# Loading memory tiles by SyncE all at once, and a one-hot operand in two small buffers, in a hybrid decoder layer

## The chip, the cores and the metric

The kernel runs on one core of a Trainium2 chip. The metric is the device time of one execution in microseconds (us). The engines are TensorE (PE; its weight loads are PEld), VectorE (DVE), ScalarE (ACT), GpSimd (POOL) and SyncE (SP). SP only issues transfers here; POOL issues some as well.

## The reference

One decoder layer on a sequence of 512 tokens with 1024 channels, in float32:

```
x = x + 0.5 * swiglu(rms_norm(x, norm_ffn1_w), ffn1_w_in, ffn1_w_out)
x = x + hybrid_mixer(rms_norm(x, norm_mix_w), ...)      # SSD heads and differential attention
x = x + memory_cross_attention(rms_norm(x, norm_cross_w),
                               rms_norm(mem, norm_mem_w), w_cq, w_ck, w_cv, w_co)
x = x + 0.5 * swiglu(rms_norm(x, norm_ffn2_w), ffn2_w_in, ffn2_w_out)
return rms_norm(x, norm_final_w)

swiglu(h, w_in, w_out): gate, up = split(h @ w_in);  (silu(gate) * up) @ w_out      # width 2816
attention bias:         rel_bias[rel_bucket(rel)]    # rel_bias: 32 buckets x 8 heads
```

`mem` is a fixed memory of 256 tokens with 1024 channels. Two things that the mixer and the cross-attention need long after the first feed-forward are prepared during it: the attention bias as a function of distance, and the RMS norm of the memory tokens.

## The kernel before

Tokens lie along the free dimension and channels along the 128 partitions: `x` is 8 tiles of 128 x 512. Each float32 operand of a large product is split into a high part (`...h`, made by ACT, L149 or L153) and a low part (`...l`, made by DVE, L150 or L154), and each product is three matmuls (L140, or L218 in the quads). A weight tile (`wr`, 128 x 1024, 512 KB) is loaded by SP into one of 6 buffers and split into `wh` and `wl`, of which there are 3 each.

A feed-forward (`ffn`) works in three thirds of 8, 8 and 6 hidden tiles. Each third has an input part, which makes two gate and two up tiles at a time (`quad`: seven products `qa`, `qb`, `qe` from five loaded weight tiles, two of which POOL completes by a transfer that accumulates, L226), and an output part: for each of 8 output tiles one weight tile, 3 matmuls for each hidden tile into `po`, and two DVE instructions that add the result to `x` (L448, L449). Hidden tiles end as `gh` and `gl`, by way of `gate`, `th` and ACT's and DVE's L393 to L398. The two hidden pairs of the last quad are ready only some time after the first matmuls of the output part begin.

The order of the program is written by `Order`: a dense stream of matmul work, and side chains that are woven into it by an estimate of PE's time (`od.t`); a chain's `yield n` puts its next step n us of that estimate later. When an output part of the first feed-forward begins, `beside` starts side chains: in the middle third `prepare` (the bias table and small constants) and `memory_norm`; in the last third `memory_prep`, which makes the scaled and split memory `hm` for the keys. Much later `out_attn` starts `memory_prep` again, for the values.

The order on SP is the order of the program text (`manual_schedule(engines={SP})`). For the other engines a planner orders the instructions when the program is built: it takes, by the order of the text, the first that it believes ready. On the chip each engine then runs its own list in that order and waits where it must. `issue_after`, and the helper `behind` around it, put an instruction behind a named one on its engine.

Small tiles come from one pool with two tags: tiles of more than 256 columns take one of 56 buffers (`s2`), others one of 14 (`s1`):

```
def s2(s, dt=F32, shape=(P, T)):
    if math.prod(shape[1:]) <= T // 2:
        return sp.tile(list(shape), dt, tag="s1", name=nm(s), bufs=NHALF)
    return sp.tile(list(shape), dt, tag="s2", name=nm(s))
```

`prepare` (L486 to L514) loads `lamv`, `rel_sb` (the 32 x 8 bias values) and `hot` (32 x 512, one-hot rows that pick a bucket for each distance) by SP. After 7.5 us of the estimate it multiplies them on PE (`prel`, 8 x 512), copies the result over `hot` on ACT (L511), stores it by POOL to `rel_d` (L512) and has POOL write it 128 times to `rel_z` (L514), from which each attention head reads its bias.

`memory_tile` (L870) loads one 128 x 256 tile of the memory by POOL, behind the last accumulating transfer of the text. `memory_norm` loads such a tile, squares it on ACT (`nacc`, `nsq`) and adds the square on DVE (L339), 8 times with 2 us between; `finish` then makes the norm with small matmuls `nps` and `nrow`. `memory_prep` loads each tile again and splits it into `hm`.

Of the kernel before, what the change touches and what calls it, by code (L numbers as in the profile page):

```python
# [13 lines left out]
AF = mybir.ActivationFunctionType  # L14
# [4 lines left out]
T = 512  # L19
D = 1024  # L20
KT = D // P
# [6 lines left out]
NUM_BUCKETS = 32  # L28
# [66 lines left out]
def body(tc, a, dbg=None):  # L95
    nc = tc.nc
# [12 lines left out]
    def nm(s):  # L109
        uid[0] += 1  # L110
        return f"{s}_{uid[0]}"
# [5 lines that stand above are left out]
# [4 lines left out]
    def small(s, n, bufs=None):  # L121
        return tiny.tile([P, n], F32, tag=s, name=nm(s), bufs=bufs)

    def acc(s, shape=(P, T)):
        return acc_p.tile(list(shape), F32, tag="acc", name=nm(s))

    def aux(s, shape=(P, T)):
        return aux_p.tile(list(shape), F32, tag="aux", name=nm(s))
# [5 lines left out]
    last, start, last_sum, recent = [], [], [], []  # L134
    V, S, G = nc.vector, nc.scalar, nc.gpsimd
    od = Order()

    def mm(out, w, x, start, stop):
        od.t += (1 if w.dtype == R32 else 4) * (x.free_size() + 8) / 2400
        nc.tensor.matmul(out, w, x, start=start, stop=stop)  # L140
# [16 lines left out]
    def split(s, src, scale=None, half=False, n=T):  # L157
        if half:
            both = s2(s, R32, (P, 2, T // 2))
            hi, lo = both[:, 0], both[:, 1]  # L160
        else:
            hi, lo = s2(s + "h", R32, (P, n)), s2(s + "l", R32, (P, n))
        last[:] = [i.ins for i in split_into(hi, lo, src, scale)]
        return hi, lo

    def load_w(src, n=D):
        raw = wp.tile([P, n], F32, tag="wr", name=nm("wr"), bufs=6)
        nc.sync.dma_start(raw, src)
        hi = wp.tile([P, n], R32, tag="wh", name=nm("wh"))
        lo = wp.tile([P, n], R32, tag="wl", name=nm("wl"))  # L170
        with ExitStack() as after:
            for i in start:
                after.enter_context(tc.issue_after(i))
            recent[:] = [i.ins for i in split_into(hi, lo, raw)]
        return hi, lo

    @contextmanager
    def behind(ins):
        with ExitStack() as after:
            for i in ins:  # L180
                after.enter_context(tc.issue_after(i))
            yield

    H = T // 2
# [87 lines left out]
    def proj(ps, w, xs, ks=None):  # L272
        n = len(xs)
        for k in ks or range(n):
            mm3(ps, w, xs[k], k == 0, k == n - 1, wc=slice(k * P, (k + 1) * P))
            yield
# [187 lines left out]
    def beside(ti):  # L464
        if ti == 1:
            od.spawn(prepare())
            od.spawn(memory_norm())
        elif ti == 2:
            od.spawn(memory_prep(hm))

    def fin1(o):
        st_mix.add(x[o])
# [2 lines left out]

    od.spawn(st1.finish(), 18.0)
    od.add(ffn(h1, [], st1, a["f1q"], [a["f1o0"], a["f1o1"], a["f1o2"]], fin1, wa_s, a["f1i"], at_out=beside))


# [3 lines left out]
    rel_d = dram.tile([8, RW], F32, name="rel_d")  # L483
    rel_z = dram.tile([8, P, RW + 1], F32, name="rel_z")

    def prepare():  # L486
        lamv = cp.tile([P, 4, 64], F32, name="lamv")
        yield 0.0
        nc.sync.dma_start(lamv, a["lam"].partition_broadcast(P))
        lamp = small("lamp", 64, bufs=2)  # L490
        lsum = small("lsum", 2, bufs=1)
        for j in range(2):
            V.tensor_tensor(lamp, lamv[:, 2 * j, :], lamv[:, 2 * j + 1, :], ALU.mult)
            V.reduce_sum(lsum[:, j : j + 1], lamp, axis=AX.X)
        lexp = small("lexp", 2, bufs=1)
        G.tensor_tensor(lexp, euler[:, 0:1].to_broadcast([P, 2]), lsum, ALU.pow)
        V.tensor_tensor(nlam, lexp[:, 1:2], lexp[:, 0:1], ALU.subtract)
        V.tensor_scalar(nlam, nlam, -LAMBDA_INIT, None, ALU.add)
        V.tensor_scalar(wsub, par[:, C_SUBLN : C_SUBLN + 1], 1.0 - LAMBDA_INIT, None, ALU.mult)
        V.tensor_scalar(dskh, par[:, C_DSKIP : C_DSKIP + 8], 0.5, None, ALU.mult)  # L500
        rel_sb = s2("rel_sb", shape=(NUM_BUCKETS, 8))
        nc.sync.dma_start(rel_sb, a["rel_bias"])
        hot = s2("hot", shape=(NUM_BUCKETS, T))
        nc.sync.dma_start(hot, a["hot"])
        rel_far = s2("rel_far", shape=(8, RW - T))
        V.memset(rel_far, MASKED)
        nc.gpsimd.dma_start(rel_d[:, T:], rel_far)
        yield 7.5
        prel = aux("prel", (8, T))
        mm(prel, rel_sb, hot, True, True)  # L510
        S.activation(hot[:8], prel, AF.Copy, scale=-8.0)  # L511
        nc.gpsimd.dma_start(rel_d[:, :T], hot[:8])  # L512

        nc.gpsimd.dma_start(rel_z[:, :, :RW], rel_d[:, None, :].to_broadcast([8, P, RW]))  # L514

# [187 lines left out]

    def out_attn(hg, o0, o1, prep=False):
        if prep:
            od.spawn(memory_prep(hm2), 0.0)
        yield lambda: all(y is not None for y in ya[4 * hg : 4 * hg + 4])
        heads = ya[4 * hg : 4 * hg + 4]
        for o in range(o0, o1):
            po = acc("pm")  # L710
            yield from proj(po, load_w(a["woa"][hg, o], 4 * P), heads)
            V.tensor_tensor(x[o], x[o], po, ALU.add)
        if o1 == KT:
            ya[4 * hg : 4 * hg + 4] = [None] * 4
# [152 lines left out]
    st_mem = Stat(MEM)  # L867
    ck, cv = [], []

    def memory_tile(k):  # L870
        mk = s2("mem", shape=(P, MEM))
        with behind(last_sum):
            nc.gpsimd.dma_start(mk, a["memT"][k])
        return mk

    def memory_norm():
        for k in range(KT):
            mk = memory_tile(k)
            with behind(recent):
                st_mem.add(mk)  # L880
            yield 2.0
        yield 3.0
        yield from st_mem.finish(6.0)

    def memory_prep(dst):
        for k in range(KT):
            mk = memory_tile(k)
            with behind(recent):
                dst.append(split("hm", mk, par[:, C_MEM + k : C_MEM + k + 1], True))
            yield 2.0  # L890
# [51 lines left out]
    hm, hm2 = [], []  # L942
# [4 lines left out]
    for hd in range(1, 4):  # L947
        od.add(queries_keys(hd))
    od.add(group_dense(0))
    od.add(out_attn(0, 0, 8))  # L950
    od.add(values(1))
    for hd in range(4, 8):
        od.add(queries_keys(hd))
    od.add(group_dense(1))
    od.add(out_attn(1, 0, SPLIT))
    od.add(group_dense(2))
    od.add(group_dense(3))
    od.add(out_attn(1, SPLIT, 8, True))
    od.add(memory_values())
    od.add(out_proj(ys, a["wos"], lambda: all(y is not None for y in ys), upd_c))  # L960
# [221 lines left out]
```

## Time and profile before

| | |
|---|---|
| median of 3 runs | 1351.1 us (1350.3 to 1351.55) |
| the profiled execution, whole | 1348.26 us |
| the profiled execution, span from first to last instruction | 1346.1 us |
| mean granted clock of TensorE | 0.998 |
| PE busy | 1321.8 us, 98% |
| DVE, ACT, POOL busy | 950.7, 631.2, 114.0 us |
| the 8 loads of `wr` of the middle third's output part, first and last issue on SP | 194.5 and 233.0 us |
| `hot`: issue of its load; its store to `rel_d`; `rel_z` | 195.9; 231.1; 233.5 us |
| memory tiles, POOL: first load of the norm; first of `hm` | 198.3; 314.2 us |

Every row of the trace is from the one profiled execution. A timeline row gives the start, the duration, the engine, the line, the operation and the tiles it writes and reads; in brackets stands the idle time of that engine before it and what ended it. A row of waits gives a total, a count and the longest. Matmuls are pipelined: the next begins before the last has ended, and their ends are modelled.

### The profile page before, as it was taken

The numbers are of one execution on the slowest core, as the hardware profiler recorded it, in microseconds if no ns is written. First come the engines' busy times: TensorE is split into PE (matmuls) and PEld (weight loads), VectorE is DVE, ScalarE is ACT, GpSimd is POOL, SyncE is SP. The second block draws the span as 40 slices with busy tenths as digits, with TensorE's granted clock in tenths as the row PEclk, the third lists the DMA queues.
The fourth block names the chain that finished last, engine by engine and source line by source line (L and its number), as shares of the span: only waits on it lengthen the run. The fifth ranks groups of instructions, "written<-read, shape, count | busy, mean of one in ns | idle before, by whom it ended". The sixth has DMA issues, their size and how long they took to land.

```text
span 1346.1 us, 19858 instructions
## 1 busy us (share of the span) xinstructions
PE 1321.8 (98%) x7829; PEld 1148.1 (85%) x7829; DVE 950.7 (71%) x1480; ACT 631.2 (47%) x1069; POOL 114.0 (8%) x138
## 2 busy tenths in 40 slices
PE   8999998999999999999999999999999999999997
PEld 7888997889897778877788887889889989998996
DVE  6774787467895586657867877656788757875774
ACT  6442454145553474446654555434445424542453
POOL 1000011111020001100011031000011000000000
PEclk9999999999999999999999999999999999999999
DMA  7434574756442314432162574322347655745641
GB/s 268 111 119 128 128 198 121 229 126 184 126 150 80 99 33 83 138 96 67 45 132 84 92 137 146 110 78 64 81 113 182 174 129 126 200 140 125 172 111 62
DMA packets 50540, 167.89 MB, mean 125 GB/s; under 512 B 6592, under 2 KB 7000, under 8 KB 50448
## 3 DMA queue, kind: packets, MB, share of 16 engines
q1 hardware_dynamic: 40704, 134.57, 31.8%
q0 software_dynamic: 9744, 32.06, 14.2%
q8 instruction: 61, 1.00, 0.3%
q14 instruction: 31, 0.25, 0.1%
HBM read 164.45 MB, written 4.77 MB: 126 GB/s over the span
## 4 chain that ended last, share of the span: by engine, by line
PE 88%; DVE 4%; DMA 2%; ACT 2%; issue 1%; POOL 1%; POOLq 0%; SPq 0%; ACTq 0%; DVEq 0%
PE po L140 16%; PE qb L218 11%; PE pm L140 8%; PE qe L218 7%; PE qa L218 7%; PE pxbc L140 7%; PE pk L140 3%; PE pq L140 3%; PE pcq L140 3%; PE pv L140 3%; PE pz L140 3%; PE pf L140 2%; PE pg L140 2%; PE pu L140 2%; PE ps L140 2%; DMA r<-cum_d 2%
## 5 line engine op out<-in xcount | busy, mean ns | idle before, releaser
L149 ACT ACTIVATE wh<-wr 128x1024 fp32r<-128x1024 f32 (+2 forms) x285 | 292.1, 1027 | 384.0 <-PE po L140 117.9
L150 DVE TENSOR_TENSOR wl<-wr,wh 128x1024 fp32r<-128x1024 f32 (+2 forms) x285 | 337.6, 1185 | 101.1 <-ACT wh L149 98.8
L140 PE MATMUL po<-gh,wh 128*128 128x512 f32 x304 | 118.6, 392 | 2.8 <-ACT wh L149 1.6
L140 PE MATMUL po<-gh,wl 128*128 128x512 f32 x304 | 118.0, 390 | 0.5 <-DVE wl L150 0.5
L140 PE MATMUL po<-gl,wh 128*128 128x512 f32 x304 | 118.2, 390 | 0.2 <-DVE gl L150 0.2
L218 PE MATMUL qa<-hmh,wl 128*128 128x256 f32 x304 | 86.3, 284 | 0.1
L218 PE MATMUL qa<-hml,wh 128*128 128x256 f32 x304 | 86.1, 283 | 0.0
L218 PE MATMUL qa<-hmh,wh 128*128 128x256 f32 x304 | 86.0, 283 | 0.0
L448 DVE TENSOR_TENSOR upd<-po,row 128x512 f32<-128x512 f32 x40 | 27.6, 691 | 78.6 <-PE po L140 78.3
L140 PEld LDWEIGHTS po<-gh,wh 128*128 128x128 f32 x304 | 56.8, 188 | 17.3 <-ACT gh L149 3.2
L140 PEld LDWEIGHTS po<-gl,wh 128*128 128x128 f32 x304 | 57.1, 188 | 12.9 <-DVE gl L150 1.3
L140 PEld LDWEIGHTS po<-gh,wl 128*128 128x128 f32 x304 | 57.1, 188 | 12.5 <-DVE wl L150 1.0
L218 PEld LDWEIGHTS qa<-hmh,wl 128*128 128x128 f32 x304 | 58.3, 192 | 0.7 <-DVE wl L150 0.7
L218 PEld LDWEIGHTS qa<-hml,wh 128*128 128x128 f32 x304 | 58.3, 192 | 0.2
L218 PEld LDWEIGHTS qa<-hmh,wh 128*128 128x128 f32 x304 | 58.3, 192 | 0.2
L140 PE MATMUL pxbc<-hnh,wh 128*128 128x512 f32 x128 | 52.3, 408 | 0.0
L140 PE MATMUL pxbc<-hnl,wh 128*128 128x512 f32 x128 | 50.3, 393 | 0.0
L140 PE MATMUL pxbc<-hnh,wl 128*128 128x512 f32 x128 | 50.2, 393 | 0.0
L226 POOL DMA_DIRECT2D wr<-in_f2q x22 | 19.2, 871 | 362.3 <-DVE wl L150 86.7
L636 ACT ACTIVATE ec<-ec,mn 128x512 f32<-128x512 f32 (+3 forms) x64 | 35.4, 555 | 25.2 <-DVE mn L635 25.2
L218 PE MATMUL qe<-s12h,wh 128*128 128x256 f32 x152 | 43.4, 286 | 3.2 <-ACT wh L149 1.9
L149 ACT ACTIVATE gh<-th 128x512 fp32r<-128x512 f32 x38 | 23.1, 624 | 45.7 <-DVE th L396 45.7
(375 smaller groups left out, 3808.0 us busy)
## 6 DMA issues: line engine op xcount, KB each, us to landing
wr<-in_f2q SPq DMA_DIRECT2D x55, 512.0 KB, 3.9
wr<-in_f1q SPq DMA_DIRECT2D x40, 512.0 KB, 4.3
wr<-in_f2q POOLq DMA_DIRECT2D x22, 512.0 KB, 6.3
wr<-in_f2o SPq DMA_DIRECT2D x22, 512.0 KB, 4.4
wr<-in_f1q POOLq DMA_DIRECT2D x16, 512.0 KB, 5.8
wr<-in_f1o SPq DMA_DIRECT2D x16, 512.0 KB, 4.2
wr<-in_wxbc SPq DMA_DIRECT2D x16, 512.0 KB, 3.5
wr<-in_f1i SPq DMA_DIRECT2D x8, 512.0 KB, 6.9
```

The source lines that it names most:

```text
L140: nc.tensor.matmul(out, w, x, start=start, stop=stop)
L149: S.activation(hi, src, AF.Copy),
L150: V.tensor_tensor(lo, src, hi.bitcast(F32), ALU.subtract),
L218: nc.tensor.matmul(out, a_[:, wc], b_, start=first and f == 0 and kp == 0 and j == 0, stop=kp == n - 1 and j == 2, skip_group_check=True)
L226: last_sum[:] = [G.dma_start(raw, m, accum_op=ALU.add).ins]
L448: V.tensor_tensor(upd, po, row4, ALU.mult)
L636: S.activation(ec[:, :n], ec[:, :n], AF.Exp, bias=mn, scale=-1.0, accum_out=sm[c][:, i : i + 1])
```

## The change

`memory_tile` takes the issuing queue as an argument and no longer stands behind the last accumulating transfer. `memory_norm` loads all 8 tiles by SP before its first step, then waits 2 us of the estimate ahead of each square instead of behind it. `memory_prep` loads all 8 by SP at its start when it is called in the last third (`early`); at its later call it loads one at a time by POOL as before, without the place behind the accumulating transfer. `hot` becomes two tiles of 32 x 256, which by their size take the tag `s1`; product, copy and store are made for each half, and `rel_z` is written once both are stored.

```diff
@@ beside
-            od.spawn(memory_prep(hm))
+            od.spawn(memory_prep(hm, True))
@@ prepare
-        hot = s2("hot", shape=(NUM_BUCKETS, T))
-        nc.sync.dma_start(hot, a["hot"])
+        hot = [s2("hot", shape=(NUM_BUCKETS, H)) for _ in range(2)]
+        for i in range(2):
+            nc.sync.dma_start(hot[i], a["hot"][:, i * H : (i + 1) * H])
...
         prel = aux("prel", (8, T))
-        mm(prel, rel_sb, hot, True, True)
-        S.activation(hot[:8], prel, AF.Copy, scale=-8.0)
-        nc.gpsimd.dma_start(rel_d[:, :T], hot[:8])
+        for i in range(2):
+            mm(prel[:, i * H : (i + 1) * H], rel_sb, hot[i], True, True)
+        for i in range(2):
+            S.activation(hot[i][:8], prel[:, i * H : (i + 1) * H], AF.Copy, scale=-8.0)
+            nc.gpsimd.dma_start(rel_d[:, i * H : (i + 1) * H], hot[i][:8])
@@ out_attn
-            od.spawn(memory_prep(hm2), 0.0)
+            od.spawn(memory_prep(hm2, False), 0.0)
@@ memory
-    def memory_tile(k):
+    def memory_tile(k, queue):
         mk = s2("mem", shape=(P, MEM))
-        with behind(last_sum):
-            nc.gpsimd.dma_start(mk, a["memT"][k])
+        queue.dma_start(mk, a["memT"][k])
         return mk
 
     def memory_norm():
-        for k in range(KT):
-            mk = memory_tile(k)
+        mem = [memory_tile(k, nc.sync) for k in range(KT)]
+        for mk in mem:
+            yield 2.0
             with behind(recent):
                 st_mem.add(mk)
-            yield 2.0
         yield 3.0
         yield from st_mem.finish(6.0)
 
-    def memory_prep(dst):
+    def memory_prep(dst, early):
+        mem = [memory_tile(k, nc.sync) for k in range(KT)] if early else []
         for k in range(KT):
-            mk = memory_tile(k)
+            mk = mem[k] if early else memory_tile(k, G)
```

## The prediction

> **What bounds the kernel now.** The first view is the page. TensorE (PE) carries the span.
>
> ```profile
> span 1346.1 us, 19858 instructions
> PE 1321.8 (98%) x7829; PEld 1148.1 (85%) x7829; DVE 950.7 (71%) x1480; ACT 631.2 (47%) x1069; POOL 114.0 (8%) x138
> ```
>
> PE is idle for 1346.1 - 1321.8 = 24.3 us. A change that only moves loads and small copies can win no more than the part of this idle time that lies in its own stages, plus PE's own slow restarts there. The second view is the table of windows: two output parts and two runs of quads, each cut from the end of one stage to the end of the next. After the stage's bounds stand its length, PE's busy time and records, then PEld, DVE, ACT, POOL, clock, DMA share and GB/s.
>
> ```profile
> 221.83:270.99 49.16, 45.65 (x196) 35.88 (x196) 24.03 (x30) 11.62 (x14) 7.05 (x10) 1.00 0.58 173
> 1073.13:1117.02 43.89, 43.88 (x195) 35.88 (x194) 24.48 (x29) 10.65 (x12) 2.60 (x3) 1.00 0.52 131
> 270.99:336.87 65.88, 62.57 (x512) 61.50 (x511) 50.32 (x59) 32.46 (x43) 9.32 (x13) 1.00 0.57 156
> 1117.02:1177.50 60.48, 60.48 (x507) 60.48 (x506) 47.41 (x50) 30.24 (x36) 4.32 (x5) 1.00 0.65 167
> ```
>
> Rows 1 and 2 are the same work, the output part of a full third, in the first and the second feed-forward; only the first has the bias table and the memory norm beside it. It takes 49.16 - 43.89 = 5.27 us more: 49.16 - 45.65 = 3.51 us of idle PE and 45.65 - 43.88 = 1.77 us of extra busy time. Rows 3 and 4 are three quads each; here the first feed-forward loses 5.40 us: 3.31 us idle and 2.09 us extra busy. The clock column is 1.00 in all four, so no throttle is in this. The third view is who PE waited for from 221 to 336 us (total, times, longest):
>
> ```profile
> PE qe L218 <- ACT wh L149: 1.9, 1, 1.9
> PE po L140 <- ACT wh L149: 1.6, 1, 1.6
> PE po L140 <- ACT gh L149: 1.1, 1, 1.1
> PE qe L218 <- DVE wl L150: 0.8, 1, 0.8
> PE qb L218 <- DVE wl L150: 0.5, 1, 0.5
> PE po L140 <- DVE wl L150: 0.5, 1, 0.5
> PE po L140 <- DVE gl L150: 0.2, 1, 0.2
> ```
>
> Seven waits, and they are all the idle time of both stages: the `po` rows sum to 3.4 us (output part), the `qe` and `qb` rows to 3.2 us (quads). All end on splits made by ACT and DVE, none on a DMA. So the question is why ACT split late. The fourth view is ACT's timeline, first around the output part that begins at 221.83, then at the same place in the second feed-forward (1073.13):
>
> ```profile
> 209.73 1.04 ACT L149 ACTIVATE wh<-wr 128x1024 fp32r<-128x1024 f32 x1
> ...
> 215.98 1.06 ACT L149 ACTIVATE wh<-wr 128x1024 fp32r<-128x1024 f32 x1 [1.82 <-PE qb L218]
> 216.94 0.40 ACT L335 ACTIVATE nacc<-mem 128x256 f32<-128x256 f32 x1
> 217.25 0.40 ACT L338 ACTIVATE nsq<-mem 128x256 f32<-128x256 f32 x1
> 222.64 1.06 ACT L393 ACTIVATE th<-gate 128x1024 f32<-128x1024 f32 x1 [4.99 <-DVE gate L392]
> 226.38 1.15 ACT L149 ACTIVATE gh<-th 128x512 fp32r<-128x512 f32 x2 [2.67 <-DVE th L396]
> 230.20 0.59 ACT L511 ACTIVATE hot<-prel 8x512 f32<-8x512 f32 x1 [2.67 <-PE prel L140]
> 230.70 1.04 ACT L149 ACTIVATE wh<-wr 128x1024 fp32r<-128x1024 f32 x1
> ```
>
> ```profile
> 1070.17 1.06 ACT L149 ACTIVATE wh<-wr 128x1024 fp32r<-128x1024 f32 x1 [1.82 <-PE qe L218]
> 1073.05 1.06 ACT L149 ACTIVATE wh<-wr 128x1024 fp32r<-128x1024 f32 x1 [1.82 <-PE qb L218]
> 1074.02 1.04 ACT L393 ACTIVATE th<-gate 128x1024 f32<-128x1024 f32 x1
> ```
>
> In the second feed-forward ACT goes on splitting weight tiles at every product's end until `th` runs at 1074.02; PE then has a second output tile to work on while the last two `g` tiles are made. In the first, after the split at 215.98 (weight tile 0) ACT stands idle for 4.99 us and splits tile 1 only at 230.70, behind the copy `hot<-prel`. The tile was there: SP issued it at 197.35, right behind `hot`.
>
> ```profile
> 195.32 0.43 SPq L502 DMA_DIRECT2D rel_sb<-in_rel_bias  x1
> 195.85 0.36 SPq L504 DMA_DIRECT2D hot<-in_hot  x1
> 197.35 0.35 SPq L168 DMA_DIRECT2D wr<-in_f1o  x1
> ```
>
> So this is an order fixed when the program was built, not a late transfer. SP's order is written by hand; those of ACT, DVE, PE and POOL come from the planner, which takes the first instruction that it believes ready. It believed `hot` and the tile behind it to come late. My reading: tiles of one tag get their buffers in program order, `hot` has the large tag, and its turn comes only after the `gh` and `gl` of the last quad (226 to 228 us). On the chip the buffer was free at 195.85; in the plan SP stood still there. The last view is POOL:
>
> ```profile
> 201.82 1.17 POOL L873 DMA_DIRECT2D mem<-in_memT  x2
> 231.08 0.53 POOL L512 DMA_DIRECT2D rel_d<-hot  x1 [28.09 <-ACT hot L511]
> 231.60 0.56 POOL L873 DMA_DIRECT2D mem<-in_memT  x1
> 233.55 1.10 POOL L514 DMA_DIRECT2D rel_z<-rel_d  x1 [1.39 <-DMA rel_d<-hot]
> ```
>
> POOL stood 28.09 us before the store of `hot`, and memory tile 3 and all later ones stood behind it (231.60 and on). The last four squares therefore fell into the first quad of the next third:
>
> ```profile
> 273.90 0.58 ACT L248 ACTIVATE qb<-qa 128x512 f32<-128x512 f32 x1 [12.91 <-PE qa L218]
> 274.39 0.41 ACT L338 ACTIVATE nsq<-mem 128x256 f32<-128x256 f32 x1
> 274.70 1.05 ACT L149 ACTIVATE wh<-wr 128x1024 fp32r<-128x1024 f32 x1
> ```
>
> **The change part by part.** (1) `hot` in two halves of the small tag, which has 14 buffers: 2 `hot`, `rel_sb`, `rel_far` and 8 memory tiles are 12, and `nacc` and one `nsq` make 14, so SP finds a buffer for each load at once, and later squares wait for one add of `nacc` at most. `hot` no longer queues behind the last quad's tiles. I expect ACT to split tiles 1 and 2 ahead of `th`, as in the second feed-forward. This removes the 3.51 us of idle time. PE's extra busy time there is 1.77 us, of which the table's product has 1.0:
>
> ```profile
> L140 PE MATMUL prel<-hot,rel_sb 32*8 32x512 f32 x2 | 1.0, 589 | 0.0
> ```
>
> The other 0.77 us are slow first matmuls after each wait and go with the waits: together -4.28 us. If the waits stay, 0.
>
> (2) The product in two halves: the same columns through PE in twice the instructions. Its cost is between 0 (time by columns) and +1.0 us (each half as dear as a whole); nearest is the whole's own 1.0 us, which is mostly streaming, so I take +0.1. ACT makes a second copy (at most the 0.59 of the whole) and POOL a second store (at most 0.53): `rel_z` starts up to 1.1 us later. Its first reader is the bias load of the first attention head, after the whole last third, so not before 336.87 (row 3 of the windows): nothing on the path.
>
> (3) Memory tiles, 8 at the first call and 8 at the second, leave POOL for SP and stand between weight tiles 0 and 1 of their output part.
>
> Eight tiles of 128 x 256 floats are 1.05 MB. Queued behind them on SP is weight tile 1 and all later ones. SP's issues of small tiles stand about 0.5 us apart (195.32 and 195.85), so eight take 4 us, and the bytes take 1.05 MB / 253 GB/s = 4.1 us at the rate of the first row here (bounds, length, clock, DMA share, GB/s):
>
> ```profile
> 194.00:200.00 6.00, 1.00 0.85 253
> 206.00:212.00 6.00, 1.00 0.14 25
> ```
>
> Tile 1 would be issued near 201 instead of 197.35; its own 512 KB take 2 us at that rate, and with the 4.1 us ahead of it it lands near 208. ACT can take it one product of PE after the split at 215.98, at about 218.9 (2.88 us, the step from 1070.17 to 1073.05). Some ten us of cover hide it; the DMA engines are nearly empty from 206 to 212 (second row). If the cover were gone, 4 us. On POOL the accumulate of the last quad's fifth tile, split at 209.73, runs beside these loads and may land up to 4.1 us later. Its product begins here (critical chain):
>
> ```profile
> 213.18 2.88 PE qb L218 x24
> ```
>
> The split ends at 210.77 on ACT and, with as much again for DVE's half, near 212; 1.2 us of slip are free, and the cost lies between 0 and 4.1 - 1.2 = +2.9; I take 0, because the DMA engines fall idle from 206 on, so most of the slip is made up. At the second call the same loads stand in the same place of SP's order, and PE is busy throughout that output part today: 0.
>
> ```profile
> 336.87:370.00 33.13, 33.13 (x148) 27.01 (x147) 28.11 (x43) 17.03 (x27) 0.00 (x0) 1.00 0.41 126
> ```
>
> [...]
>
> (4) Squares and adds of the memory norm, 2 us later in the plan but with data present: all eight move into the output part, where ACT is busy 11.62 of 49.16 us. The `nsq` at 274.39 no longer stands before the split at 274.70 (0.3 us), and DVE loses its adds of `nacc` there: between 0 and the 3.31 us of idle time of the quads; I take 0.5, because the larger cause, `qb<-qa` ahead of that split, is not touched for certain. The norm's own matmuls on PE move with it and cost the same.
>
> Sum: -4.28 + 0.1 - 0.5 = -4.7 us. The profiled execution took 1348.26 us (span 1346.1 and 2.2 around it); the median of the three runs is 1351.1, 0.2% above. A difference in PE's idle time carries over to either, so 1351.1 - 4.7 = 1346.4 us.
>
> **The rivals.** Both stages heal: the split at 274.70 stands behind `qb<-qa` because the planner believes the accumulate of the quad's second tile late, behind `rel_z` and a memory tile on POOL. With the memory tiles gone, and if the earlier `hot` lets the product run in a gap of the last quads so that `rel_z` starts sooner, the quads also run without waits: 3.31 instead of 0.5, and some 0.6 of restarts (0.77 went with four waits, here there are three): -4.28 + 0.1 - 3.9 = -8.1, 1343.0 us. For it: the quads from 1117.02 have no idle time at all. Against it: `rel_z` may start when it does now.
>
> No change: the cause of the late split is another than the buffer of `hot` (for that: SP issued it at 195.85 with no visible wait), or the planner still holds tile 1 late. Then 3.51 us of waits stay and only the 0.5 and 0.1 count: 1350.7 us.
>
> Slower: one mechanism, weight tile 1 behind eight memory loads. If the planner reckons these loads slow enough that tile 1 comes to it after the start of `po`, ACT's order puts its split behind the copies and the squares, and PE stands as in the second row of the waits, but longer. It decides once the split is planned later than today's 230.70; the price is the 4.1 us of bytes or 4 us of issues ahead of it, with the 0.1 and the 0.5: +3.7, 1354.8 us. For it: 4 us more stand in front of a tile that was late already. Against: the 10 us of cover.
>
> **How the numbers follow.** Forecast (1346.4) 0.34; both heal (1343.0) 0.27; no change 0.23; slower 0.16. A measurement here can tell 0.2%, 2.7 us, from no change. The first two are faster by more than that, 0.61; no change gives 0.23; slower 0.16. The range goes from 1342.6, just under the second case, to 1352.5, which takes in no change with 1.8 us of the accumulate's slip; it leaves out the slower case and a little on either side, about 0.2.
>
> **What would show it.** Right: in the output part of the middle third, splits of tiles 1 and 2 before `th`, no PE wait on `wh` or `gh`, the stage at 44.5 to 46.5 us (the norm's matmuls now within); `prel` in twice the instructions for about 1.1 us; all memory loads on SP within 5 us near 196; eight squares before 260. In the first quad of the last third either `qb<-qa` still ahead of the split (forecast) or behind it (both heal). Wrong: a split of tile 1 that still follows the copy of `prel`; SP waiting before a memory load; or waits of PE on `wh` after 290 that are not there today.

## The result, and the profile after

The changed kernel took 1341.48 us (median of nine runs, 1339.06 to 1346.57); nine runs of the kernel before had a median of 1349.21 us (1346.61 to 1353.36). The ratio is 0.9947, with an interval of 0.9927 to 0.9967: 7.7 us less between the medians. The forecast was 4.7 us less. Of the 4.9 us between 1346.4 and 1341.48, 1.9 are the starting point (1351.1 from three runs, 1349.21 from nine); 3.0 are the effect. One of the executions below, of the run with the memory part alone, took 1855.58 us at a mean clock of 0.654 and is left out of its ratio.

The profiled execution after took 1342.28 us. The page, in the lines that answer to the first two of before:

```profile
span 1340.4 us, 19873 instructions
PE 1321.4 (99%) x7831; PEld 1149.7 (86%) x7831; DVE 951.1 (71%) x1480; ACT 631.5 (47%) x1070; POOL 104.0 (8%) x123
```

The span lost 5.7 us and PE's busy time only 0.4. The windows of the three stages, each cut at the first matmul of the next (length, PE's busy time, then PEld, DVE, ACT, POOL, clock, DMA share, GB/s):

```profile
222.76:267.18 44.42, 44.42 (x199) 36.34 (x197) 24.26 (x34) 11.07 (x15) 1.60 (x2) 1.00 0.49 156
267.18:332.16 64.98, 62.56 (x507) 62.14 (x506) 49.05 (x54) 31.16 (x38) 5.03 (x6) 0.97 0.63 165
332.16:365.14 32.98, 32.98 (x146) 26.88 (x145) 28.03 (x42) 16.84 (x26) 0.00 (x0) 1.00 0.41 126
```

The output part of the middle third went from 49.16 to 44.42 us and has no idle time left. The quads went from 65.88 to 64.98, with a clock of 0.97 where it was 1.00. PE's waits from 221 to 336 us are two instead of seven:

```profile
PE qe L218 <- ACT wh L149: 1.7, 1, 1.7
PE qe L218 <- DVE wl L150: 0.8, 1, 0.8
```

ACT's timeline at the start of that output part shows the cause of the first gain: weight tiles 0, 1 and 2 are split at 217.08, 219.96 and 222.84, one at the end of each product, all ahead of `th`.

```profile
217.08 1.06 ACT L149 ACTIVATE wh<-wr 128x1024 fp32r<-128x1024 f32 x1 [1.82 <-PE qb L218]
218.05 0.40 ACT L335 ACTIVATE nacc<-mem 128x256 f32<-128x256 f32 x1
219.96 1.06 ACT L149 ACTIVATE wh<-wr 128x1024 fp32r<-128x1024 f32 x1 [1.51 <-PE qe L218]
220.93 0.71 ACT L338 ACTIVATE nsq<-mem 128x256 f32<-128x256 f32 x2
222.84 1.07 ACT L149 ACTIVATE wh<-wr 128x1024 fp32r<-128x1024 f32 x1 [1.21 <-PE qb L218]
223.81 1.04 ACT L393 ACTIVATE th<-gate 128x1024 f32<-128x1024 f32 x1
```

SP issued the loads as forecast, and POOL, which had stood 28.09 us before the store of `hot`, now stands 5.49; PE multiplies the table in the last quad, in four instructions and 1.03 us (two and 1.0 before):

```profile
196.57 0.88 SPq L505 DMA_DIRECT2D hot<-in_hot  x2
197.50 5.58 SPq L875 DMA_DIRECT2D mem<-in_memT  x8
```
```profile
204.43 1.03 PE L140 MATMUL prel<-hot,rel_sb 32*8 32x256 f32 x4
```
```profile
208.19 1.09 POOL L515 DMA_DIRECT2D rel_d<-hot  x2 [5.49 <-ACT hot L514]
```

In the first quad of the last third no square is left, but `qb<-qa` still stands ahead of the split on which PE waits 1.7 us:

```profile
270.25 0.58 ACT L248 ACTIVATE qb<-qa 128x512 f32<-128x512 f32 x1 [12.92 <-PE qa L218]
270.74 0.38 ACT L350 ACTIVATE row<-nrow 128x256 f32<-128x256 f32 x1
271.00 1.06 ACT L149 ACTIVATE wh<-wr 128x1024 fp32r<-128x1024 f32 x1
```

Behind that wait the clock falls (2 us windows, columns as above):

```profile
270.00:272.00 2.00, 0.45 (x4) 0.24 (x3) 0.00 (x0) 1.75 (x3) 1.60 (x2) 1.00 0.33 33
272.00:274.00 2.00, 1.13 (x5) 0.92 (x6) 1.87 (x2) 0.06 (x1) 0.00 (x0) 0.76 1.00 182
274.00:276.00 2.00, 2.00 (x11) 2.00 (x11) 0.82 (x2) 1.33 (x2) 0.00 (x0) 0.50 1.05 201
276.00:278.00 2.00, 2.00 (x17) 2.00 (x17) 2.00 (x2) 1.04 (x2) 0.00 (x0) 0.89 0.58 113
278.00:280.00 2.00, 2.00 (x19) 2.00 (x18) 2.00 (x3) 1.19 (x2) 0.00 (x0) 1.00 0.04 8
```

Missing clock times length, (0.24 + 0.50 + 0.11) x 2, is 1.7 us. In the stages of the layer's traces drops came to 1.7 us or to two or three times that (1.70 in the quads of the run with `hot` alone, 3.42 with the halves alone, 5.1 with the squares put back). Below, "less a drop" means that all of it is taken off: these quads took 64.98 - 1.70 = 63.3 us, and 65.88 before, where no drop fell. That is a lower bound: by my reading a late split catches up while the matmuls are slow. The run with the memory part alone (below) has the same matmuls in the same order in these quads, and no drop: it takes 64.21 us. So this drop cost about 0.8 us here, not 1.7, and the quads gained 65.88 - 64.21 = 1.67 us, not 2.6.

### The profile page after: what moved, and what is told of

It is laid out like the page before. It is cut to its first block, busy times and chain, and to the rows that moved or that the text cites. A ratio compares the mean times of both kernels' runs of the same rounds, so it can differ in the third digit from the quotient of the medians.

```text
span 1340.4 us, 19873 instructions
## 1 busy us (share of the span) xinstructions
PE 1321.4 (99%) x7831; PEld 1149.7 (86%) x7831; DVE 951.1 (71%) x1480; ACT 631.5 (47%) x1070; POOL 104.0 (8%) x123
## 4 chain that ended last, share of the span: by engine, by line
PE 91%; DVE 3%; DMA 1%; ACT 1%; issue 1%; POOL 1%; POOLq 0%; ACTq 0%; DVEq 0%
PE po L140 17%; PE qb L218 12%; PE qe L218 8%; PE pm L140 8%; PE qa L218 8%; PE pxbc L140 7%; PE pk L140 3%; PE pq L140 3%; PE pcq L140 3%; PE pv L140 3%; PE pz L140 3%; PE pf L140 2%; PE pg L140 2%; PE pu L140 2%; PE ps L140 2%; DMA r<-cum_d 1%
## 5 line engine op out<-in xcount | busy, mean ns | idle before, releaser
L218 PE MATMUL qe<-s12h,wl 128*128 128x256 f32 x152 | 43.8, 288 | 0.8 <-DVE wl L150 0.8
```

The costliest lines, as they stand in the source:

```text
L218: nc.tensor.matmul(out, a_[:, wc], b_, start=first and f == 0 and kp == 0 and j == 0, stop=kp == n - 1 and j == 2, skip_group_check=True)
```

## The experiments

Theory A: the plan holds `hot` until the buffers of the large tag have gone round, and with it the loads behind it on SP, so the split of weight tile 1 is planned late. Rival B: the memory tiles on POOL, stuck behind the store of `hot`, are to blame. Theory C: the split in the first quad is planned late because its tile's accumulate stands behind `rel_z` on POOL. The plan itself is not recorded: what it held is inferred from the order that each engine then ran.

**`hot` alone, with a buffer of its own.** The kernel before, and only the buffer changed (one large buffer fewer pays for it):

```diff
-NSLOT = 56
+NSLOT = 55
-        hot = s2("hot", shape=(NUM_BUCKETS, T))
+        hot = sp.tile([NUM_BUCKETS, T], F32, tag="hot", name=nm("hot"), bufs=1)
```

> Kernel before with one edit: hot stays one tile of 512 columns but has a buffer of its own (the large tag has 55 instead of 56); memory tiles stay on POOL. Theory A (the plan held hot, and the weight tiles behind it on SP, until hot's turn for a buffer of the large tag came): the output part of the middle third loses its 3.5 us of idle time and comes to 43.9 to 44.5 us instead of 49.16; the whole is 4 to 5 us faster than before. Rival B (the memory tiles on POOL and their squares made the splits late): the output part stays near 49 us and the time within 1 us.

Measured: 1344.19 us against 1350.55, ratio 0.9958 (0.9942 to 0.9975). The output part and the quads:

```profile
223.30:267.24 43.94, 43.93 (x195) 35.89 (x193) 22.14 (x27) 9.54 (x10) 5.95 (x9) 1.00 0.63 182
267.24:334.48 67.24, 63.92 (x511) 62.91 (x510) 52.31 (x62) 33.52 (x45) 8.43 (x13) 0.97 0.57 156
```

No idle time in the output part, with all memory tiles still on POOL. The quads, less a drop of 1.70, take 65.54: hardly a gain there. The whole gained 6.4 us, more than the 4 to 5 expected; the stages give 5.2, less 0.3 for the table's product in the quads before.

**`hot` in halves alone.** The kernel before with the change's edits to `prepare` and nothing else.

> Kernel before with the hot part of the change alone: two halves in small buffers, memory tiles still by POOL. Theory A: as with a buffer of its own, output part 43.9 to 44.5 us, 4 to 5 us faster. If the halving itself matters (more instructions, or the small tag filling up), it differs from the kernel with a buffer of its own by over 1 us. Rival B: output part near 49 us.

Measured: 1344.55 us against 1350.55, ratio 0.995 (0.9934 to 0.9966); output part 43.89 us, quads 68.25 less two drops of 3.42 together, 64.83. For the output part it does not matter which buffer `hot` gets, only that it has one free. In this trace the quads before the output part took 83.27 us, 1.5 more than with a buffer of its own, with a PE wait of 1.1 us on a small tile (`nlam`); the medians of the two runs differ by 0.4 us only.

**The memory part alone.** The changed kernel with `hot` as before.

```diff
-        hot = [s2("hot", shape=(NUM_BUCKETS, H)) for _ in range(2)]
+        hot = s2("hot", shape=(NUM_BUCKETS, T))
...
```

> The change without its hot part: memory tiles by SP all at once, hot one tile of the large tag. Theory A: the wait of SP for hot stays in the plan, so the output part keeps 3 to 4 us of idle time and 48.5 to 50 us; only the squares leave the quads, gain 0.5 to 1.5 us. Rival B: the output part comes to 44.5 us and the gain is 4 us or more.

Measured: 1348.58 us (1348.32 without the execution of 1855.58) against 1350.55, ratio 0.9983 (0.9966 to 1.0), so the time alone does not tell it clearly from the kernel before. Output part and quads, then ACT at the start of the output part:

```profile
222.26:273.86 51.60, 47.79 (x201) 37.48 (x199) 26.14 (x36) 13.41 (x20) 3.29 (x4) 0.97 0.45 144
273.86:338.07 64.21, 61.55 (x507) 60.92 (x506) 49.02 (x54) 31.05 (x38) 5.04 (x6) 1.00 0.67 167
```
```profile
216.58 1.06 ACT L149 ACTIVATE wh<-wr 128x1024 fp32r<-128x1024 f32 x1 [1.82 <-PE qb L218]
223.25 1.06 ACT L393 ACTIVATE th<-gate 128x1024 f32<-128x1024 f32 x1 [5.61 <-DVE gate L392]
...
230.81 0.59 ACT L511 ACTIVATE hot<-prel 8x512 f32<-8x512 f32 x1 [2.67 <-PE prel L140]
...
231.61 1.04 ACT L149 ACTIVATE wh<-wr 128x1024 fp32r<-128x1024 f32 x1
```

The split of tile 1 still follows the copy of `prel`, as before. Rival B falls, and A stands. But the quads, without a drop, take 64.21: the memory part is worth 1.67 us there, where I had put 0.5. Of the third wait of before, 0.5 us on `wl`, this row is left:

```profile
283.42 0.39 PE L218 MATMUL qa<-hmh,wh 128*128 128x256 f32 x1 [0.23 <-ACT wh L149]
```

And the old waits of the output part cost a drop in this trace (51.60 - 1.72 = 49.88), which they did not in the one I forecast from.

**The squares put back.** The changed kernel, the loads untouched, with the last four squares ordered behind `qb<-qa` of the first quad:

```diff
-        for mk in mem:
-            yield 2.0
-            with behind(recent):
+        for k, mk in enumerate(mem):
+            yield 40.0 if k == 4 else 2.0
+            with behind(recent if k < 4 else mark):
...
-        S.activation(b_ps, a_ps, AF.Copy)
+        mark[:] = [S.activation(b_ps, a_ps, AF.Copy).ins]
```

> The changed kernel with the loads as they are, but the last four squares of the memory norm ordered behind the copy qb<-qa of the last third's first quad, where the kernel before had them. Theory: these squares and the end of the norm behind them are what the quads gained by the memory part of the change; the quads take 65 to 66.5 us (63.3 in the changed kernel, 65.9 before; stretches of low clock taken out), the output part stays at 43.9 to 44.5, and the median is 1.5 to 3 us above the changed kernel's. Rival: it was the loads leaving GpSimd, not the squares; then the quads stay at 63.3 us and the median does not move.

Measured: 1345.15 us, against 1343.27 for the changed kernel and 1350.49 for the kernel before on the same chip; ratio to before 0.9958 (0.9941 to 0.9975). The quads, and PE's waits in both stages:

```profile
266.76:337.50 70.74, 65.41 (x511) 64.53 (x510) 51.98 (x59) 32.49 (x42) 4.81 (x6) 0.93 0.55 144
```
```profile
PE nps L140 <- DVE nacc L339: 3.0, 1, 3.0
PE nrow L140 <- DVE ndiag L322: 1.8, 1, 1.8
PE qe L218 <- DVE wl L150: 0.5, 1, 0.5
```

The quads take 65.6 us less drops (63.3 in the changed kernel) and have 5.3 us of waits instead of 2.4, on the squares' sum (`nacc`) and the end of the norm. The forecast number came, but by other waits than those of the kernel before: it had none on `nacc`, none on `ndiag` of this length, and the wait on `wh` is gone here. So the run shows that the place of the squares alone can cost the quads this much; it does not rebuild what the kernel before lost, and does not rule out the rival, the loads. (Low clock that lay in the 5.3 us of idle time is taken off with the rest, so the 65.6 is a lower bound.)

**Four other places for `rel_z`.** First behind the accumulate on POOL:

```diff
+        yield 50.0
+        with behind(last_sum):
-        nc.gpsimd.dma_start(rel_z[:, :, :RW], ...)
+            nc.gpsimd.dma_start(rel_z[:, :, :RW], ...)
```

> The changed kernel with the 2.6 MB write rel_z put behind the accumulating transfers of the next quad on POOL (50 us later in the plan). Theory C (the first quad of the last third waits because the plan believes the accumulate of its second tile late behind rel_z): the 2.4 us of idle time of the quads go, the quads come to 61 to 62.5 us instead of 65 (60.5 and the norm's matmuls), and the whole is 2.5 to 4 us faster than the changed kernel. Rival D (the norm's row copy and POOL's wait for the norm make the split late): the idle time stays at 2 us or more and the time is that of the changed kernel within 1 us.

Measured: 1343.81 us against 1350.55, ratio 0.9957 (0.9938 to 0.9976). In the first quad the split now runs before `qb<-qa` and PE does not wait, as C says. But the quads keep 4.2 us of idle time and take 64.17 us less two drops, so C's numbers (no idle time, 61 to 62.5 us, 2.5 to 4 us faster than the changed kernel's 1341.48) did not come. The second quad has a wait of 3.8 us on `wh`, and ACT shows why:

```profile
288.98 1.06 ACT L393 ACTIVATE th<-gate 128x1024 f32<-128x1024 f32 x1 [5.55 <-DVE gate L392]
291.13 0.58 ACT L248 ACTIVATE qb<-qa 128x512 f32<-128x512 f32 x1 [1.09 <-PE qa L218]
292.72 1.15 ACT L149 ACTIVATE gh<-th 128x512 fp32r<-128x512 f32 x2 [1.01 <-DVE th L396]
293.77 1.04 ACT L149 ACTIVATE wh<-wr 128x1024 fp32r<-128x1024 f32 x1
```

ACT idles 5.55 us before `th` while the split stands behind `th`, the copy and both `gh` in its list; POOL had issued that tile's accumulate at 283.02. My reading, not tested by itself: the second quad's accumulates now follow `rel_z` in the plan, so their tile is believed late there.

Then `rel_z` on SP, so that no accumulate stands behind it:

```diff
-        nc.gpsimd.dma_start(rel_z[:, :, :RW], ...)
+        nc.sync.dma_start(rel_z[:, :, :RW], ...)
```

> The changed kernel with the broadcast rel_z issued by SyncE instead of GpSimd. Theory: the copy qb<-qa stands ahead of the split in the first quad because the plan holds the accumulate of the second weight tile behind rel_z on GpSimd; with rel_z gone from that queue the split comes first, no PE wait on wh or wl is left in the last third's quads, they take 60.5 to 61.5 us instead of 63.3 (stretches of low clock taken out), and with fewer gaps for the clock to fall in the median is 2.5 to 4 us below the changed kernel's. Rival: the lateness only moves on, as in the run with rel_z behind the accumulate, where PE then waited 3.8 us in the second quad; quads 63 to 65 us and the same median. Second rival: SyncE waits for the stores of the table ahead of rel_z and weight tiles 2 and on come late: PE waits on wh in the output part, 46 us or more instead of 44.4.

Measured: 1339.55 us, 1343.27 for the changed kernel beside it; ratio to before 0.9907 (0.9888 to 0.9926). Output part and quads:

```profile
222.71:269.84 47.13, 45.18 (x201) 36.42 (x199) 27.37 (x39) 12.29 (x17) 4.16 (x5) 1.00 0.67 184
269.84:330.31 60.47, 60.47 (x505) 60.47 (x504) 46.26 (x49) 29.95 (x36) 2.59 (x3) 1.00 0.59 161
```

The quads take 60.47 us, as in the second feed-forward (60.48): `rel_z` on POOL was the cause of the wait. By which way is not shown. In this run and the three others of this group the end of the norm moved as well: ACT made `row` at 259.65 us here and at 257.06 to 257.80 in the others, against 270.74 in the changed kernel, where it stood right ahead of the late split. So the accumulate (C) and the norm's copy (rival D of the run before) are not told apart. The second rival holds as well: tile 2 stood behind `rel_z` on SP (8 x 128 x 640 floats, 2.6 MB), ACT waited 5.26 us for its load, and the output part is 47.13.

```profile
233.88 1.06 ACT L149 ACTIVATE wh<-wr 128x1024 fp32r<-128x1024 f32 x1 [5.26 <-DMA wr<-in_f1o]
```

Then `rel_z` on SP behind the quads' tiles (`yield 80.0` ahead of it):

> As the run with rel_z on SyncE, but with rel_z issued only behind the weight tiles of the last third's quads, so that no weight tile of either stage stands behind it. Theory: PE has no wait in the output part of the middle third nor in the quads behind it; 43.9 to 44.5 us and 60.5 us; nothing else moves, since the first reader of rel_z comes after the last output part; median 2 to 3 us below the run with rel_z on SyncE and about 6 below the changed kernel's, 1336 to 1338 us. Rival: rel_z is 2.6 MB and now lies ahead of the last output part's tiles on SyncE; if they come late PE waits there, 35 us or more instead of 33.0, and the time is no better than with rel_z on SyncE (1339.5).

Measured: 1345.13 us, far from the 1336 to 1338 expected, against 1350.59; ratio 0.9959 (0.9946 to 0.9971). Output part 44.64; PE does not wait inside the quads, but 6.49 us at their end, for the first weight tile of the next output part, whose split has moved behind `th` and `gh`:

```profile
329.44 1.06 ACT L393 ACTIVATE th<-gate 128x1024 f32<-128x1024 f32 x1 [8.48 <-DVE gate L392]
333.18 1.15 ACT L149 ACTIVATE gh<-th 128x512 fp32r<-128x512 f32 x2 [2.67 <-DVE th L396]
334.23 0.83 ACT L149 ACTIVATE wh<-wr 128x768 fp32r<-128x768 f32 x1
```

The rival named the place; on the chip SP had issued the tile at 302.09. And last, `rel_z` on SP amid the output part's tiles (`yield 20.0`):

> The changed kernel with rel_z on SyncE between the fifth and the sixth of the output part's late weight tiles (of eight), so that the tiles behind it have two or three products of PE before they are needed, and no tile of the next output part stands behind it. Theory: both earlier placements failed only by the tile that stood right behind rel_z; here the output part takes 43.9 to 44.6 us and the quads 60.5, the last output part 33.0, PE waits on no split from 221 to 365 us, and the median is 1336 to 1338.5 us, below the first placement on SyncE (1339.5). Rival: 2.6 MB ahead of two tiles and of the first quad's five again push one of them late; then PE waits on wh near the end of the output part or in the first quad and the time is 1339 or more.

Measured: 1339.23 us; the changed kernel beside it 1340.25 (below); ratio to before 0.9921 (0.9903 to 0.994). Quads 60.48, but the output part 48.76, with a drop of 1.72 and two waits. The time is above the 1336 to 1338.5 expected. The cause is neither the theory's nor the rival's: ACT stood 16.23 us at the norm's `row`, with three splits behind it.

```profile
257.06 0.38 ACT L350 ACTIVATE row<-nrow 128x256 f32<-128x256 f32 x1 [16.23 <-PE nrow L140]
257.34 2.94 ACT L149 ACTIVATE wh<-wr 128x1024 fp32r<-128x1024 f32 x3
```

The first and the last placement on SP are at or just under the changed kernel, by 3.7 and 1.0 us between medians of six; the intervals of their ratios to before overlap with the changed kernel's, so neither is shown to beat it.

**The changed kernel again.** Twice more, beside the runs above.

> The changed kernel itself, on the chip of the next runs, for comparison. Its span is read stage by stage after taking out the stretches in which the granted clock was below 1.00; in the profiles so far each such stretch costs 1.7 us or twice that. Expected: output part of the middle third 44.4 us, quads of the last third 63.3 us without such stretches, PE waits of 1.7 and 0.8 us in the first quad; median 1341 to 1344 us. If the gain of the first comparison were mostly luck of the clock, it is above 1345.

Measured: 1343.27 us against 1350.49, ratio 0.9933 (0.9913 to 0.9953); output part 44.39, quads 66.37 less two drops of 3.42 together, 62.95.

> The changed kernel once more on the same chip, as the measure for the run beside it: median 1341 to 1344 us; without stretches of low clock the output part 44.4 and the quads 63.0 to 63.3 us.

Measured: 1340.25 us against 1349.12, ratio 0.9934 (0.991 to 0.9958); output part 44.41, quads 65.14 less 1.70, 63.44. The median is just under the 1341 to 1344 expected. The gain comes again both times, so it is not mostly luck of the clock; how much of it the clock gives is worked out below.

**Gaps and the clock.** Two kernels that compute nothing of the layer, one execution of each: dense runs of matmuls (128x512), gaps between them made by chains of ACT copies.

> Not the layer: only 99 dense runs of 40 to 55 matmuls (128x512, 9 to 12 us) with a gap behind each, made by a chain of ScalarE copies on which the next run waits; eleven lengths of gap from about 0.5 to 4.5 us, nine times each in random order. Read: after which gaps the granted clock falls, and for how long. [...] Second rival: the drops have nothing to do with gaps and fall anywhere.

> Not the layer: dense runs of matmuls and gaps as in the ladder of gaps, with seven kinds of gap, fourteen times each: single ones of about 1.7, 1.9 and 2.1 us, and pairs with two matmuls (0.5 us) between them, about 1.7 and 0.75, 1.25 and 1.25, 1.0 and 1.0, 0.64 and 0.64 us. In the ladder no gap up to 1.73 us lowered the clock, while 7 of 9 of 2.2 to 2.3 us did; in the layer it fell behind a pair of 1.67 and 0.76 us. [...] Rival: only one unbroken gap counts; then no pair lowers the clock. [...]

One drop of the ladder: the matmuls with the gap before them, then the clock in 2 us windows.

```profile
388.96 12.78 PE L80 MATMUL ps<-h,wr 128*128 128x512 f32 x48 [2.28 <-ACT h L85]
```
```profile
388.00:390.00 2.00, 1.04 (x4) 0.90 (x5) 0.88 (x2) 0.00 (x0) 0.97 0.00 0
390.00:392.00 2.00, 2.00 (x6) 1.53 (x5) 0.00 (x0) 0.00 (x0) 0.50 0.04 8
392.00:394.00 2.00, 2.00 (x8) 1.60 (x7) 0.00 (x0) 0.00 (x0) 0.68 0.00 0
```

The missing clock adds to (0.03 + 0.50 + 0.32) x 2 = 1.7 us. Counted over both kernels:

| gap, us | drops behind it |
|---|---|
| 0.37 to 1.57 | 0 of 53 |
| 1.67 to 1.73 | 0 of 23 |
| 1.77 to 1.83 | 7 of 14 |
| 2.06 to 2.12 | 7 of 14 |
| 2.22 to 2.28 | 7 of 9 |
| 2.5 | 5 of 9 |
| 2.86 to 3.2 | 6 of 9 |
| 3.95 to 4.01 | 9 of 9 |
| pair 0.64 and 0.64, 0.5 of matmuls between | 1 of 13 |
| pair 1.0 and 1.0 | 5 of 14 |
| pair 1.25 and 1.25 | 9 of 14 |
| pair 1.73 and 0.75 | 8 of 14 |

No drop stood behind the 76 single gaps of 0.37 to 1.73 us, and 9 of 9 had at least one at 3.95 to 4.01; in between it was 5 to 7 of each 9 or 14. Of the pairs, those of 1.0 us and more had a drop in 5, 9 and 8 of 14 cases, though no gap in them is longer than 1.73 us: the rival that only one unbroken gap counts is out (the one drop at 0.64 and 0.64 stands by itself; its second gap had grown to 0.92). Drops that fall anywhere are out as well, by the same 76. What in the chip brings a drop about is not shown.

## Why the prediction was wrong

The largest term, the output part, was right in mechanism and size. The time came out below the range because the quads' term (4) was priced by the wrong rows, a term for the clock was missing, and the base was high.

(1) "Together -4.28 us" for the output part: right. It lost 4.74 us, and 0.33 of it came back in the quads before (81.44 to 81.77 us), where the table's product went: -4.4. The runs with `hot` alone show it by itself (43.94 and 43.89 us), and the run without it shows the old waits.

(2) +0.1 for the halves: 1.03 us in four instructions for 1.0 in two. Right.

(3) 0 for the loads on SP: right. No tile came late, and the last output part took 32.98 us (33.13). Eight issues took 5.58 us, against the estimate of 4.

(4) "The norm's own matmuls on PE move with it and cost the same", and the 0.5 us taken for the rest: this step failed. Without a drop the quads gained 1.67 us. Most of it is the norm's own matmuls, which in the kernel before stood amid the quads' products:

```profile
283.67 0.60 PE L140 MATMUL nps<-ones,nacc 128*128 128x1 f32 x4
287.78 0.86 PE L140 MATMUL nrow<-ndiag,ones_r 128*128 128x256 f32 x2
```

The quads' matmuls follow each other every 0.12 us (283.22, 283.34, 283.46). By the starts of the matmuls around these two rows (283.46 to 284.34 us for two of the quads' matmuls, 287.57 to 288.47 for one), `nps` cost the quads 0.64 us and `nrow` 0.78: 1.4 of the 2.09 us of extra busy time in the second view. The other 0.7 lie, in the main, at the three waits (by the starts of that trace): the first matmul behind each is followed after 0.22 us instead of 0.12 (275.80 to 276.02, 277.06 to 277.28, 280.73 to 280.95), and the last ahead of each counts as busy for its whole 0.28 us, 0.16 more than its step; that is an estimate of 3 x 0.26 = 0.8. In the changed kernel `nps` stands in the output part, for about 0.5 us (44.42 us with it, 43.94 without it in the run with `hot` alone), and `nrow` fills a stretch in which PE has nothing else to do, so it costs nothing:

```profile
270.05 0.40 PE L140 MATMUL nrow<-ndiag,ones_r 128*128 128x256 f32 x2
272.12 0.39 PE L218 MATMUL qe<-s12h,wh 128*128 128x256 f32 x1 [1.67 <-ACT wh L149]
```

What I did price, the `nsq` of 0.3 us ahead of the split, gained almost nothing: `row<-nrow` took its place there (270.74 us, 0.38 long), and from the last `qa` matmul to the first of `qe` PE takes 2.19 us (269.93 to 272.12) against 2.22 before (273.58 to 275.80). The reason for keeping the number small was true: `qb<-qa` stands ahead of that split still.

(5) A term was missing. "The clock column is 1.00 in all four, so no throttle is in this" was true of one execution. In others the old waits had drops of 1.7 us behind them, as the memory part alone showed in the output part. Over the 66 runs of the kernel before beside the experiments and all 21 of the changed kernel, the mean time fell from 1350.6 to 1341.9 us; the mean of (1 - mean clock) x time fell from 6.3 to 4.5. So about 1.8 us of 8.7 are fewer drops, and 6.9 are left; the stages give 4.4 + 1.7 = 6.1. Where the other 0.8 us lie stays open. Against that mean the base of 1351.1 is only 0.5 us high; the nine runs of the first comparison, with their median of 1349.21, are the low ones.

The rival "both stages heal" had nearly the measured time (1343.0), but by luck: its mechanism did not come. Its condition came true, since `rel_z` started at 211.72 us instead of 233.55 and no memory tile was left on POOL, and yet the wait of the quads stayed. "No change" and "slower" fell with the first profile.

## What to carry to other kernels

An order fixed at build time follows what the planner believes: one small tile waiting its turn for a large-tag buffer, or one 2.6 MB transfer on a queue, put splits of tiles that had long landed behind work that waits, and moving the transfer only moved the place. When small matmuls leave a stage, price them by what they cost where they stand: the same `nrow` took 0.78 us amid dense products and nothing inside a wait. And a PE wait may cost more than itself, which one profile may or may not show: in the two kernels of gaps a drop of 1.7 us stood behind 7 of 14 gaps of 1.77 to 1.83 us, 9 of 9 of 3.95 to 4.01 and 9 of 14 pairs of 1.25 us. When stages of two traces are compared, a drop cannot simply be taken off: the one of 1.7 us in the quads here cost 0.8.

## What was not expected of the hardware

The granted clock of this single core fell behind short waits of PE, in some cases and not in others. In the profile after it read 0.76, 0.50 and 0.89 in the 2 us windows from 272 to 278 us, behind waits of 1.67 and 0.76 us, and 1.7 us of clock were missing; in the profile before it stayed at 1.00 behind waits of 1.94 and 0.76 us in the same quad (274 to 280 us). In the kernels of gaps 7 of 14 gaps of 1.77 to 1.83 us and 7 of 9 of 2.22 to 2.28 us had a drop behind them, and pairs of 1.25 us in 9 of 14 cases.

One wait changed from run to run with no edit near it: `py` on `r` (late in the mixing part, with `r` loaded by a transfer) took 1.89 us in the profile before (814.23), 1.85 in the profile after (808.78), and 0.19 in the second repeat of the changed kernel (808.23). In the first two the clock drops at that place, too: 0.60 and 0.54 in the 2 us windows from 814 to 818 us before, 0.73 and 0.50 from 808 to 812 after.
